# Units of two head pairs over 256 tokens in a delta-rule recurrence, with the triangular inverse's steps on GpSimd

## The chip, the core and the metric

The kernel runs on one core of one Trainium2 chip. The metric is the device time of one execution in microseconds (us). TensorE (PE) multiplies matrices, VectorE (DVE) and ScalarE (ACT) work element by element and evacuate PSUM, GpSimd (POOL) works on SBUF alone here, and SyncE (SP) issues nearly all DMAs, in the order of its queue.

## The reference, cut to what matters

One transformer block over 1024 tokens of width 1024: a modulated norm, one wide projection `u @ w_in`, two mixers (softmax attention with forget gates, 8 heads of 64; and a delta-rule recurrence, "RWKV-7", 8 heads of 64), gates, an output projection and a convolutional FFN. The change touches the recurrence alone:

```python
def step(state, inp):                      # per head: state is 64 x 64
    r_t, w_t, k_t, v_t, a_t, b_t = inp     # a = -kk, b = kk * a_h, kk normalised per head
    sa = jnp.einsum('bhvk,bhk->bhv', state, a_t)
    state = state * w_t[:, :, None, :] + sa[..., None] * b_t[:, :, None, :] + v_t[..., None] * k_t[:, :, None, :]
    y_t = jnp.einsum('bhvk,bhk->bhv', state, r_t)
    return state, y_t
...
_, y = lax.scan(step, state0, ...)         # over 1024 tokens
y = groupnorm(y) * ln_w + ln_b
return (y + sum(r * k * r_k) * v) * g
```

## The kernel before

Everything is held as (channel, token): 128 partitions are two heads (a pair p, p = 0 to 3), and a tile is 128 x 512 (512 tokens, half hf = 0 or 1). The recurrence is cut into chunks of 64 tokens (CH). Inside a chunk it becomes a few small products and the inverse of a unit triangular 64 x 64 matrix; between chunks only the 64 x 64 state is carried on. Eight chunks of one pair (512 tokens, NCU = 8) make a unit, and there are 8 units, (p, hf) with hf inner.

`pre` (L814) readies a unit. It loads the decays (`cum`) and rates (`al`), takes the key norm by a product with a block matrix (`head_sums`, L779: the upper part `hi` is rounded on ACT, the lower part `lo` subtracted on POOL at L782, then two 512 wide matmuls), scans and exponentiates the decays (`el`, `en`), forms the operands `ar` and `bk`, multiplies them into the chunk matrices (`p`, masked into `E` at L878), and sends the 32 x 32 diagonal blocks through DRAM (`sm`) into `M32`, with 128 blocks on 128 partitions. `inverse` (L787) then solves all of them at once: 31 steps of two element-wise VectorE instructions each, a product (L795) and a sum (L799), every one needing the one before. Two DMA legs (`se`, `TT`) bring the result back.

`main` (L924) waits for that (L936 transposes `TT` on VectorE; the products `xi` and `zi` need it first on TensorE), builds `Wt`, `Zt` and `Mt`, and runs the state chain (L989 to L1002): for each of 8 chunks two matmuls of the old state into `sp`, one VectorE instruction (L996) that makes the new state S, two matmuls of the old state into `yp`. A group norm over the heads and the output follow.

The order on TensorE is written by the program itself, through a small planner (`Weave`, L48). A chain yields the time that it must wait, and the planner fills that time with plain 128 x 128 x 512 matmuls from a queue of independent work: the projections of the r, k, v of the pairs to come (`ps_rkv`), queries and keys (`qk`), values (`v`), and 16 gate tiles (`gt`, each two halves of 24 matmuls). Such an item loads its weights on SP (L258), splits them into two parts (L266 on ACT, L270 on VectorE), and its result is evacuated by ACT and VectorE (L383 for r, k and v). In the recurrence the order of the other engines is set by the scheduler. The gate tiles that the recurrence has not used go into the attention that follows (`rk_ps`), and what is left after it is run before the branch products (`br`, L1352).

The numbers that a chain yields are the planner's own: `ready` (L891) is how long after its M32 loads a unit's inverse is taken to be there, 1150 the distance of two state steps, 3400 that from `hi` and `lo` to their matmuls.

Of the kernel before, what the change touches and what calls it, by code (L numbers as in the profile page):

```python
# [9 lines left out]
F32 = mybir.dt.float32  # L10
# [125 lines left out]
def hybrid_block(ctx: ExitStack, tc: tile.TileContext, a, out):  # L136
# [223 lines left out]
    with ExitStack() as es:  # L360
# [26 lines left out]
        def rkv_items(p, hf):  # L387
            ts_ = {x: rkp.tile([128, NH], F32, tag=f"{x}{hf}", name=f"{x}{p}{hf}") for x in "rkv"}
            rkv[p, hf], got[p, hf] = [ts_[x] for x in "rkv"], 0

            def steps(w, x, t):
                if hf == 0:
                    last_col[p, x] = shp.tile([128, 1], F32, tag=f"pv{x}", name=f"pv{p}{x}")
                yield from shifted(w, t, hf, ts_[x], last_col[p, x], f"rkv{t}")
                got[p, hf] += 1

            for x, t in (("k", 4 + p), ("r", p), ("v", 8 + p)):
                yield (lambda t=t: w_in(12 + t)), (lambda w, x=x, t=t: steps(w, x, t))
# [253 lines left out]
        with tc.tile_pool(name="lg", bufs=1, reuse_waits="tile") as lg, \  # L652
# [47 lines left out]
            def lora_chain():  # L700
                yield 13000
                for p in range(4):
                    yield from lora(p, [(j, [(w2h[:, j * 512 : j * 512 + 512], xs2[j]), (w2l[:, j * 512 : j * 512 + 512], xs2[j])], None, b) for j, b in enumerate(("w0", "a0"))])
                use_ln_exp(last[0])
                prods = split_g()
                yield from forget()
                mod_out(2)
                next(mods, None), next(mods, None)
                for p in range(4):
                    yield from lora(p, [(2, prods, None, None)])  # L710
                mod_out(5)
                while got[0, 0] < 3:
                    weave.step()
                yield 0
# [47 lines left out]
            weave.first.extend([*rkv_items(0, 0), *rkv_items(0, 1)])  # L762
# [9 lines left out]

        BKS = (slice(0, 2), slice(1, 3))
# [5 lines left out]
        def head_sums(ps, x, hi, lo):  # L779

            nc.scalar.copy(hi, x)
            nc.gpsimd.tensor_tensor(lo, x, f32(hi), op=ALU.subtract)  # L782
            yield 3400
            mm(ps, blk_r, hi, start=True, stop=False)
            mm(ps, blk_r, lo, start=False, stop=True)

        def inverse(n, M32, TT, chunk_tile, tmp):  # L787
# [3 lines left out]
            t32 = tmp("t32", 256)  # L791
            for s in range(31):
                J, W = s // 4 + 1, 31 - s
                tv = t32[:, 0 : J * W].rearrange("p (j w) -> p j w", w=W)
                i = tt(tv, E32[:, 0:J, s : s + 1].to_broadcast([128, J, W]),  # L795
                   M32[:, s : s + 1, s + 1 : 32].to_broadcast([128, J, W]), op=ALU.mult)
                if s == 0:
                    behind(i)
                tt(E32[:, 0:J, s + 1 : 32], E32[:, 0:J, s + 1 : 32], tv, op=ALU.add)  # L799
# [14 lines left out]
        def pre(k, p, hf):  # L814

            n = f"{p}_{hf}"
            cs = slice(hf * NH, hf * NH + NH)
            rr, kk, vv = rkv[p, hf]
# [8 lines left out]
            nc.sync.dma_start(cum, d_lora[0, p, :, cs])  # L827
            al = tmp("al")
            nc.sync.dma_start(al, d_lora[1, p, :, cs])
            ksq = tmp("ksq")  # L830
            nc.scalar.activation(ksq, kk, AF.Square, scale=V("k_k", p))
            parts = rw.tile([128, 3, NH], F32R, tag="bk", name=f"kp{n}")
            yield 1275 if p + hf else 6000
# [12 lines left out]
            stt(kr, rn, 1e12, kk, op0=ALU.min, op1=ALU.mult)  # L846
# [8 lines left out]
            tt(ar[:, 1], c3(rr), el[:, :, 1:], op=ALU.mult)  # L855
            ts(al, al, V("k_a", p), oka[:, p : p + 1], op0=ALU.mult, op1=ALU.add)
            tt(al, al, kk, op=ALU.mult)
            tt(bk[:, :, 1, :], c3(al), c3(en), op=ALU.mult)
            pcd = chunk_tile("pcd", 3, NCU)
            nc.gpsimd.tensor_copy(pcd, el[:, :, CH])  # L860
            rkb = tmp("ksq")
            stt(rkb, rr, V("r_k", p), al, op0=ALU.mult, op1=ALU.mult)
# [26 lines left out]
            for g in range(4):  # L889
                nc.sync.dma_start(M32[g * 32 : g * 32 + 32, :, :], sm.rearrange("h c b s t -> (h c b) s t"))  # L890
            ready = weave.now + (47500 if k == 0 else 38500)  # L891
            TT = chunk_tile("TT", 2, NCU, CH)
            weave.spawn(inverse(n, M32, TT, chunk_tile, tmp), 8500)

            vt, at = gen(f"vt{n}"), gen(f"at{n}")
            for b in range(4):
                bs = slice(b * 128, b * 128 + 128)
                transpose(vt[:, bs], vv[:, bs], ident)
                transpose(at[:, bs], ar[:, 0, 2 * b : 2 * b + 2, :], ident)
# [21 lines left out]
            tt(bon, bp, vv, op=ALU.mult)  # L921
            units[p, hf] = dict(ready=ready, pcd=pcd, ar=ar, E=E, QA=QA, TT=TT, bon=bon, UV=UV)

        def main(k, p, hf):  # L924
            o = units.pop((p, hf))
            n = f"{p}_{hf}"
            cs = slice(hf * NH, hf * NH + NH)
# [52 lines left out]
            S0 = state.get(p)  # L980

            for c in range(NCU):
                alone = hf == 0 and c == 0
# [5 lines left out]
            for c in range(NCU):  # L989
                if S0 is not None:  # L990
                    for h in range(2):
                        mm(sp[HS[h], c, :], Mt[HS[h], c, :], S0[HS[h], :], start=False, stop=True, more=True)
                S1 = None
                if not (hf == 1 and c == NCU - 1):
                    S1 = rw.tile([128, CH], F32, tag="state", name=f"S{n}{c}", bufs=3)
                    ts(S1, sp[:, c, :], pcd[:, c : c + 1], None, op0=ALU.mult)  # L996
                if S0 is not None:
                    for h in range(2):
                        mm(yp[HS[h], c, :], S0[HS[h], :], Zt[HS[h], c, :], start=False, stop=True, more=True)
                if c + 1 < NCU:  # L1000
                    yield 1150
                S0 = state[p] = S1  # L1002
# [20 lines left out]
            stt(y, y, V("ln_w", p), rs, op0=ALU.mult, op1=ALU.mult)  # L1023
            stt(y, y, V("ln_b", p), bon, op0=ALU.add, op1=ALU.add)
            gg = rw.tile([128, NH], F32, tag="Wt", name=f"gg{n}", bufs=1)
            nc.sync.dma_start(gg, d_lora[2, p, :, cs])
            ov = rw.tile([128, NH], F32, tag="ysq", name=f"o{n}", bufs=1)
            tt(ov, y, gg, op=ALU.mult)
            nc.sync.dma_start(d_orw[p, :, cs], ov)
# [25 lines left out]
        order = [(p, hf) for p in range(4) for hf in range(2)]  # L1055
        passed.update((k, x) for k in (-1, -2) for x in range(2))

        def pre_chain():
            for k, (p, hf) in enumerate(order):
                while got[p, hf] < 3:  # L1060
                    weave.step()
                yield from pre(k, p, hf)
                if p < 3:
                    weave.first.extend(rkv_items(p + 1, hf))
                yield 0

        def main_chain():
            for k, (p, hf) in enumerate(order):
                while (p, hf) not in units:
                    yield 200  # L1070
                yield from main(k, p, hf)
                yield 0
# [1036 lines left out]
```

## Time and profile before

| | before |
|---|---|
| median of 3 runs (lowest to highest) | 1659.14 us (1657.43 to 1660.03) |
| the profiled execution | 1663.44 us, span 1661.7 us |
| VectorE busy | 1202.9 us, 72% |
| ScalarE busy | 809.2 us, 49% |
| GpSimd busy | 136.6 us, 8% |

The recurrence runs from about 165 us to 612 us of the span, attention from there to about 812 us, then the gates that are left, the branches and the FFN. A timeline row has the start and the length in us, the engine, the line, the operation, and what was written from what; matmuls of fp32 operands are two passes and count twice in the profile. A bracket at its end gives idle time of that engine just before, and what ended it. The end of a matmul is modelled, so rates are read from start to start.

### The profile page before, as it was taken

The numbers are of one execution on the slowest core, as the hardware profiler recorded it, in microseconds if no ns is written. First come the engines' busy times: TensorE is split into PE (matmuls) and PEld (weight loads), VectorE is DVE, ScalarE is ACT, GpSimd is POOL, SyncE is SP. The second block draws the span as 40 slices with busy tenths as digits, with TensorE's granted clock in tenths as the row PEclk, the third lists the DMA queues.
The fourth block names the chain that finished last, engine by engine and source line by source line (L and its number), as shares of the span: only waits on it lengthen the run. The fifth ranks groups of instructions, "written<-read, shape, count | busy, mean of one in ns | idle before, by whom it ended". The sixth has DMA issues, their size and how long they took to land.

```text
span 1661.7 us, 25960 instructions
## 1 busy us (share of the span) xinstructions
PE 1621.0 (98%) x9756; PEld 1329.5 (80%) x9756; DVE 1202.9 (72%) x2350; ACT 809.2 (49%) x1473; POOL 136.6 (8%) x169
## 2 busy tenths in 40 slices
PE   7999999999999998999999999999999999999998
PEld 5777877887877777887788888888888888888886
DVE  6875877887886536866579445897777777786677
ACT  7663434443446556665513144654444444555455
POOL 0010101211101020222022000000000000000000
PEclk8999999999999999999999999999999999999999
DMA  9587644443433246542487310243223223574463
GB/s 347 191 308 221 159 131 127 131 125 91 116 101 87 92 156 136 152 119 84 143 284 270 146 73 36 70 138 104 95 96 120 96 95 108 202 272 153 127 209 108
DMA packets 123902, 241.72 MB, mean 145 GB/s; under 512 B 39816, under 2 KB 48320, under 8 KB 123776
## 3 DMA queue, kind: packets, MB, share of 16 engines
q1 hardware_dynamic: 114944, 220.94, 41.1%
q0 software_dynamic: 7600, 17.25, 3.8%
q10 hardware_dynamic: 1232, 1.86, 0.4%
q8 instruction: 77, 1.26, 0.3%
q14 instruction: 49, 0.40, 0.1%
HBM read 174.43 MB, written 65.56 MB: 144 GB/s over the span
## 4 chain that ended last, share of the span: by engine, by line
PE 82%; DVE 8%; ACT 4%; DMA 3%; issue 2%; SPq 0%; POOL 0%; ACTq 0%; DVEq 0%; POOLq 0%
PE X L144 13%; PE D L144 13%; PE Y L144 6%; PE gt L144 6%; PE ps_rkv L144 5%; PE wo L144 5%; PE br L144 5%; PE W L144 3%; PE rk_ps L144 3%; PE qk L144 3%; PE v L144 3%; PE low L144 1%; PE lg L144 1%; PE ov L144 1%; PE sp L144 1%
## 5 line engine op out<-in xcount | busy, mean ns | idle before, releaser
L144 PE MATMUL D<-op,op 128*128 128x512 f32 x924 | 209.8, 390 | 0.0
L144 PEld LDWEIGHTS D<-op,op 128*128 128x128 f32 x924 | 173.4, 188 | 36.2 <-DVE op L1372 0.3
L144 PE MATMUL X<-T_m,S 128*128 128x512 f32 x440 | 107.3, 390 | 0.1
L144 PEld LDWEIGHTS X<-T_m,S 128*128 128x128 f32 x440 | 82.5, 188 | 18.2 <-ACT T_m L1797 0.6
L1371 ACT CAST op<-g 128x512 fp32r<-128x512 f32 x77 | 47.8, 621 | 72.1 <-PE D L144 48.2
L1372 DVE TENSOR_TENSOR op<-g,op 128x512 fp32r<-128x512 f32 x77 | 53.0, 689 | 40.9 <-ACT op L1371 40.8
L1608 DVE SCALAR_TENSOR_TENSOR c<-ab,vec,c 128x512 f32<-128x512 f32 x88 | 65.9, 750 | 19.5 <-ACT c L1611 17.9
L1220 DVE TENSOR_TENSOR tl<-tp,th 128x512 fp32r<-128x512 f32 (+1 forms) x80 | 50.3, 633 | 29.0 <-ACT th L1215 28.4
L1572 DVE TENSOR_TENSOR S<-ur,S 128x512 fp32r<-128x512 f32 x66 | 45.5, 691 | 35.6 <-ACT S L1568 35.4
L270 DVE TENSOR_TENSOR lo_in<-raw_in,hi_in 128x512 fp32r<-128x512 f32 x84 | 58.0, 729 | 16.4 <-PE gt L144 7.5
L1568 ACT CAST S<-ur 128x512 fp32r<-128x512 f32 x66 | 41.0, 622 | 55.6 <-DVE ur L1561 30.6
L1572 DVE TENSOR_TENSOR A<-ur,A 128x512 fp32r<-128x512 f32 x64 | 44.1, 689 | 30.9 <-ACT A L1568 30.7
L266 ACT CAST hi_in<-raw_in 128x1024 fp32r<-128x1024 f32 x42 | 43.9, 1048 | 46.1 <-PE ps_rkv L144 26.2
L795 DVE TENSOR_TENSOR t<-E,M 128x60 f32<-128x60 f32 (+24 forms) x248 | 55.0, 222 | 11.9 <-DMA M<-sm 5.9
L144 PE MATMUL Y<-T_h,A 128*128 128x512 f32 x264 | 63.5, 390 | 0.0
L144 PE MATMUL Y<-T_h,S 128*128 128x512 f32 x264 | 63.3, 390 | 0.0
L799 DVE TENSOR_TENSOR E<-E,t 128x60 f32<-128x60 f32 (+24 forms) x248 | 56.9, 230 | 5.8
L144 PE MATMUL X<-B_b,A 128*128 128x512 f32 x252 | 60.8, 390 | 0.0
L144 PE MATMUL W<-B_f,A 128*128 128x512 f32 x252 | 60.6, 390 | 0.0
L1156 ACT ACTIVATE P<-lg,nm 128x896 f32<-128x896 f32 (+3 forms) x64 | 47.4, 743 | 24.4 <-DVE nm L1147 21.2
L144 PEld LDWEIGHTS Y<-T_h,A 128*128 128x128 f32 x264 | 49.6, 188 | 10.3
L144 PEld LDWEIGHTS Y<-T_h,S 128*128 128x128 f32 x264 | 49.6, 188 | 10.3
(493 smaller groups left out, 4076.9 us busy)
## 6 DMA issues: line engine op xcount, KB each, us to landing
raw_in<-in_w_in SPq DMA_DIRECT2D x50, 512.0 KB
wm<-in_w_mod SPq DMA_DIRECT2D x48, 512.0 KB
ur<-in_w_up SPq DMA_DIRECT2D x44, 512.0 KB
g<-d_g SPq DMA_DIRECT2D x35, 512.0 KB
d_g<-gs SPq DMA_DIRECT2D x44, 256.0 KB
d_g<-c SPq DMA_DIRECT2D x33, 256.0 KB
d_st<-qh SPq DMA_DIRECT2D x64, 128.0 KB
d_gate<-gs SPq DMA_DIRECT2D x32, 256.0 KB
```

The lines of the kernel that those rows point to most:

```text
L144: weave.last = nc.tensor.matmul(o, lhsT, rhs, start=start, stop=stop, skip_group_check=more)
L266: i = nc.scalar.copy(hi, raw)
L270: nc.vector.tensor_tensor(lo[:, c : c + NH], raw[:, c : c + NH], f32(hi[:, c : c + NH]), op=ALU.subtract)
L795: i = tt(tv, E32[:, 0:J, s : s + 1].to_broadcast([128, J, W]), M32[:, s : s + 1, s + 1 : 32].to_broadcast([128, J, W]), op=ALU.mult)
L799: tt(E32[:, 0:J, s + 1 : 32], E32[:, 0:J, s + 1 : 32], tv, op=ALU.add)
L1156: nc.scalar.activation(e[:, 0:n], lg[:, 0:n], AF.Exp, bias=nm[:, 0:1], accum_out=total)
L1220: tt(tl[:, 0:w], tp[:, 0:w], f32(th[:, 0:w]), op=ALU.subtract)
L1371: nc.scalar.copy(hi, src)
L1372: tt(lo, src, f32(hi), op=ALU.subtract)
L1568: nc.scalar.copy(hi, src)
L1572: tt(lo, src, f32(hi), op=ALU.subtract)
L1608: stt(c, ab[:, x + hf * NH : x + hf * NH + NH], V("conv_w", 22 * x + i), c, op0=ALU.mult, op1=ALU.add)
```

## The change

A unit becomes two pairs (2g and 2g + 1) over 256 tokens, so that it still has 8 chunks of 64: chunks 0 to 3 of the first pair, 4 to 7 of the second. There are again 8 units, (g, quarter). Loads and stores take both pairs (two pieces of 256 columns), and instructions whose per-channel factor differs by pair are issued twice with half the width. The state chain takes both pairs in one step: 4 steps of 8 matmuls and one VectorE instruction on 128 x 128. The 62 steps of an inverse are issued to GpSimd; the lower parts in `head_sums` go to VectorE. `ready` is 50000 instead of 38500 (47500 for the first unit stays). The r, k and v tiles hold two pairs by 512 tokens, one buffer each: an item that would overwrite one holds the planner's filler back until the tile was given free.

```diff
+        free = set("krv")
+        def rkv_items(g, hf, x):
             def steps(w, p, t):
+                if p % 2 == 0:
+                    while x not in free:
+                        weave.hold = weave.now + 200
+                        yield
+                    free.remove(x)
+                    rkv[g, hf, x] = rkp.tile([128, 2, NH], F32, tag=x, name=f"{x}{g}{hf}")
...
         def head_sums(ps, x, hi, lo):
             nc.scalar.copy(hi, x)
-            nc.gpsimd.tensor_tensor(lo, x, f32(hi), op=ALU.subtract)
+            tt(lo, x, f32(hi), op=ALU.subtract)
...
             for s in range(31):
                 J, W = s // 4 + 1, 31 - s
-                i = tt(tv, E32[:, 0:J, s : s + 1].to_broadcast([128, J, W]),
+                i = nc.gpsimd.tensor_tensor(tv, E32[:, 0:J, s : s + 1].to_broadcast([128, J, W]),
                    M32[:, s : s + 1, s + 1 : 32].to_broadcast([128, J, W]), op=ALU.mult)
-                tt(E32[:, 0:J, s + 1 : 32], E32[:, 0:J, s + 1 : 32], tv, op=ALU.add)
+                nc.gpsimd.tensor_tensor(E32[:, 0:J, s + 1 : 32], E32[:, 0:J, s + 1 : 32], tv, op=ALU.add)
...
-            stt(ar[:, 0], c3(kr), nkk[:, p : p + 1], el[:, :, 0:CH], op0=ALU.mult, op1=ALU.mult)
-            stt(kr, kr, V("k_k", p), al, op0=ALU.mult, op1=ALU.mult)
+            for j, p in pairs:
+                stt(ar[:, 0, four(j)], c3(kr)[:, four(j)], nkk[:, p : p + 1], el[:, four(j), 0:CH], op0=ALU.mult, op1=ALU.mult)
+            for j, p in pairs:
+                stt(j2(kr)[:, j], j2(kr)[:, j], V("k_k", p), j2(al)[:, j], op0=ALU.mult, op1=ALU.mult)
...
-            ready = weave.now + (47500 if k == 0 else 38500)
+            ready = weave.now + (47500 if k == 0 else 50000)
...
-            for c in range(NCU):
+            for i in range(4):
                 if S0 is not None:
-                    for h in range(2):
-                        mm(sp[HS[h], c, :], Mt[HS[h], c, :], S0[HS[h], :], start=False, stop=True, more=True)
+                    for j in range(2):
+                        for h in range(2):
+                            mm(sp[HS[h], 4 * j + i, :], Mt[HS[h], 4 * j + i, :], S0[HS[h], j, :], start=False, stop=True, more=True)
...
-                    ts(S1, sp[:, c, :], pcd[:, c : c + 1], None, op0=ALU.mult)
+                    tt(S1, sp[:, i::4, :], pcd[:, i::4].unsqueeze(2).to_broadcast([128, 2, CH]), op=ALU.mult)
...
-                if c + 1 < NCU:
-                    yield 1150
+                if i < 3:
+                    yield 1300
...
-        order = [(p, hf) for p in range(4) for hf in range(2)]
+        order = [(g, quarter) for g in range(2) for quarter in range(4)]
```

The order on TensorE in the first unit's state chain, before: each `sp` and `yp` row of one pair, with plain matmuls between.

```order
453 L144 MATMUL sp_0_2294<-S_00_2364,Mt_0_2270 64x64 x2
454 L144 MATMUL yp_0_2293<-Zt_0_2269,S_00_2364 64x64 x2
455 L144 MATMUL ps_rkv_2361<-u_lo,hi_in_2249 128x512 x6
456 L144 MATMUL sp_0_2294<-S_01_2374,Mt_0_2270 64x64 x2
457 L144 MATMUL yp_0_2293<-Zt_0_2269,S_01_2374 64x64 x2
```

The same place of the change:

```order
455 L144 MATMUL sp_0_2294<-S_00_2368,Mt_0_2270 64x64 x4
456 L144 MATMUL yp_0_2293<-Zt_0_2269,S_00_2368 64x64 x4
457 L144 MATMUL qk_0_2365<-u_lo,hi_in_2249 128x512 x7
458 L144 MATMUL sp_0_2294<-S_01_2381,Mt_0_2270 64x64 x4
459 L144 MATMUL yp_0_2293<-Zt_0_2269,S_01_2381 64x64 x4
```

A step has twice the small matmuls and 7 plain ones behind it instead of 6; a unit has 4 steps instead of 8.

The queue of SP in the third unit, before: the stores of query and key tiles (`d_st`) and weight loads (`raw_in`, `raw_v`) that stand between that unit's M32 loads (row 140) and the first leg `se` behind its inverse.

```order
148 L413 DMA d_st<-qh_1_2796 64x512
149 L258 DMA raw_in_3102<-in_w_in 128x1024
150 L1026 DMA gg_1_3226<-d_lora 128x512
151 L413 DMA d_st<-qh_0_2951 64x512 x4
152 L413 DMA d_st<-ql_0_2953 64x512 x2
153 L413 DMA d_st<-qh_1_3010 64x512 x4
154 L413 DMA d_st<-ql_1_3012 64x512 x2
155 L258 DMA raw_v_3162<-in_w_v 128x1024
156 L829 DMA al_0_3426<-d_lora 128x512
157 L802 DMA se_0_2747<-E_0_2682 256x1x32 x4
```

The same unit's leg in the change, whose M32 loads are row 137:

```order
145 L420 DMA d_st<-qh_1_2876 64x512 x3
146 L420 DMA d_st<-ql_1_2878 64x512 x2
147 L420 DMA d_st<-qh_1_2876 64x512
148 L258 DMA raw_in_3093<-in_w_in 128x1024
149 L420 DMA d_st<-qh_0_2982 64x512 x4
150 L822 DMA se_2_2778<-E_2_2713 256x1x32 x4
151 L420 DMA d_st<-ql_0_2984 64x512 x2
152 L829 DMA TT_2_2562<-se_2_2778 32x8x32 x4
153 L420 DMA d_st<-qh_1_3039 64x512 x4
154 L420 DMA d_st<-ql_1_3041 64x512 x2
```

The leg stands one half item of `qk` and a weight load earlier in the queue, ahead of two rows of stores that it came after before.

The end of attention on TensorE, before: the last attention product (`ov`), the gates that are left, the first branch product.

```order
2194 L144 MATMUL ov<-tl_22_9126,vh_8515 128x256
2195 L144 MATMUL rk_ps<-u_hi,lo_in_8583 128x512 x5
2196 L144 MATMUL rk_ps<-u_hi,hi_in_8921 128x512 x8
2197 L144 MATMUL rk_ps<-u_lo,hi_in_8921 128x512 x8
2198 L144 MATMUL rk_ps<-u_hi,lo_in_8922 128x512 x8
2199 L144 MATMUL rk_ps<-u_hi,hi_in_8921 128x512 x8
2200 L144 MATMUL rk_ps<-u_lo,hi_in_8921 128x512 x8
2201 L144 MATMUL rk_ps<-u_hi,lo_in_8922 128x512 x8
2202 L144 MATMUL br_00_9270<-fx_6889,hi_br_9223 128x512
```

The same place of the change:

```order
2108 L144 MATMUL ov<-th_22_9172,vh_8570 128x256
2109 L144 MATMUL ov<-th_22_9172,vh_8570 128x128
2110 L144 MATMUL ov<-tl_22_9177,vh_8570 128x128
2111 L144 MATMUL ov<-tl_22_9177,vh_8570 128x256
2112 L144 MATMUL rk_ps<-u_hi,lo_in_8638 128x512 x2
2113 L144 MATMUL br_00_9262<-fx_6914,hi_br_9215 128x512
```

One gate tile (48 plain matmuls) that stood behind attention stands in the recurrence now: of the items' plain matmuls 1824 lie ahead of attention instead of 1776.

More of the change, by code (lines that the diff above doesn't have):

```diff
@@ L711, in lora_chain @@
                 mod_out(5)
-                while got[0, 0] < 3:
+                while min(got.get((0, 0, x), 0) for x in "krv") < 2:
                     weave.step()
@@ L979, in main @@
             sp = py.tile([128, NCU, CH], F32, tag="sp", name=f"sp{n}")
-            S0 = state.get(p)
+            S0 = state.get(g)
             for c in range(NCU):
-                alone = hf == 0 and c == 0
+                alone = quarter == 0 and c % 4 == 0
                 for h in range(2):
```

130 lines of the change are left out of this document (80 added, 50 removed).

## Prediction, on record before the run

> **What bounds the kernel now.** I read the page first: busy shares and the chain that ended last.
>
> ```profile
> span 1661.7 us, 25960 instructions
> PE 1621.0 (98%) x9756; PEld 1329.5 (80%) x9756; DVE 1202.9 (72%) x2350; ACT 809.2 (49%) x1473; POOL 136.6 (8%) x169
> PE 82%; DVE 8%; ACT 4%; DMA 3%; issue 2%; SPq 0%; POOL 0%; ACTq 0%; DVEq 0%; POOLq 0%
> ```
>
> TensorE carries the end almost alone. Next the table by stage, of which the recurrence is one row (the stretch in us, its length, then the busy time of each engine).
>
> ```profile
> core 0: us, PE busy (x) PEld busy (x) DVE busy (x) ACT busy (x) POOL busy (x), PEclk, DMA share, GB/s
> 165.00:612.00 447.00, 442.65 (x4198) 356.73 (x4198) 330.26 (x942) 205.15 (x360) 58.23 (x74) 1.00 0.41 115
> ```
>
> In the recurrence TensorE is idle 447.00 - 442.65 = 4.4 us, VectorE 117 us. So relieving VectorE is worth at most a few us there, unless TensorE's own work gets cheaper. Two waits of TensorE in this stage (us in total, times, longest):
>
> ```profile
> PE qk L144 <- DVE v L383: 2.4, 1, 2.4
> PE q L144 <- DVE QA L905: 0.4, 1, 0.4
> ```
>
> A busy TensorE can still be a slow one, so I read the timeline of a state step from start to start, the group of the stage that it belongs to (with 1.0 us of waits for the new state S), and a plain run:
>
> ```profile
> 247.52 0.33 PE L144 MATMUL sp<-S,Mt 64*64 64x64 f32 x4
> 247.68 0.28 PE L144 MATMUL yp<-Zt,S 64*64 64x64 f32 x4
> 247.90 1.67 PE L144 MATMUL ps_rkv<-u_lo,hi_in 128*128 128x512 f32 x6
> 249.50 0.33 PE L144 MATMUL sp<-S,Mt 64*64 64x64 f32 x4
> ```
>
> ```profile
> L144 PE MATMUL sp<-S,Mt 64*64 64x64 f32 x240 | 19.9, 243 | 1.3 <-DVE S L996 1.0
> ```
>
> ```profile
> 306.77 2.00 PE L144 MATMUL ps_rkv<-u_hi,lo_in 128*128 128x512 f32 x8
> 308.60 0.62 PE L144 MATMUL ps_rkv<-u_hi,hi_in 128*128 128x512 f32 x2
> ```
>
> A plain matmul costs (308.60 - 306.77) / 8 = 0.229 us. A step lasts 249.50 - 247.52 = 1.98 us: six plain ones are 1.37, the eight small passes 0.32 (0.16 a group, by the first two rows). That leaves **0.29 us a step**, in which TensorE counts as busy and nothing waits: the price of going from 128-row to 64-row matmuls and back.
>
> **The change, part by part.**
>
> *State chain.* The planner's steps with an old state are 60 now (the x240 passes of `sp<-S` are four a step) and 30 then (3 + 4 + 4 + 4 for each of two groups), each with twice the small passes. The small work stays; 30 changes of shape go: 30 x 0.29 = **-8.7 us**. Were the price one of each pair's matmuls rather than of the change of shape, it would be 0; those are the bounds. I take the whole, since the small passes themselves run at 0.04 us each, one behind the other.
>
> *Waits on VectorE.* The steps L795 and L799 leave it:
>
> ```profile
> L795 DVE TENSOR_TENSOR t<-E,M 128x60 f32<-128x60 f32 (+24 forms) x248 | 55.0, 222 | 11.9 <-DMA M<-sm 5.9
> L799 DVE TENSOR_TENSOR E<-E,t 128x60 f32<-128x60 f32 (+24 forms) x248 | 56.9, 230 | 5.8
> L270 DVE TENSOR_TENSOR lo_in<-raw_in,hi_in 128x512 fp32r<-128x512 f32 x62 | 43.7, 743 | 12.7 <-PE gt L144 7.5 <-ACT hi_in L266 3.5 <-PE ps_rkv L144 0.9
> L974 DVE TENSOR_TENSOR Zt<-mz,ar 128x256 f32<-128x256 f32 x16 | 6.7, 422 | 6.1 <-PE mz L144 5.8
> L855 DVE TENSOR_TENSOR ar<-r,el 128x512 f32<-128x512 f32 x7 | 4.8, 691 | 0.1
> L996 DVE TENSOR_SCALAR S<-sp,pcd 128x64 f32<-128x64 f32 x60 | 16.9, 281 | 19.9 <-PE sp L144 19.6
> ```
>
> That takes off 111.9 us. The 32 lower parts add 32 x 0.691 = 22 us, and the six instructions a unit that are split by pair 48 x (2 x 0.422 - 0.691) = 7 us. VectorE then has some 247 us of work in 447, so it binds less. Of the 3.8 us of waits I take **-2.5 us**: the 2.4 us came in the first unit, where VectorE stood behind the inverse's last transfer:
>
> ```profile
> 173.65 0.19 DVE L795 TENSOR_TENSOR t<-E,M 128x31 f32<-128x31 f32 x1 [5.88 <-DMA M<-sm]
> 207.78 0.17 DVE L799 TENSOR_TENSOR E<-E,t 128x8 f32<-128x8 f32 x1
> 214.16 0.43 DVE L936 STREAM_TRANSPOSE X<-TT 32x256 f32<-32x256 f32 x1 [3.81 <-DMA TT<-se]
> 216.31 1.49 PE L144 MATMUL qk<-u_hi,hi_in 128*128 128x512 f32 x4 [2.43 <-DVE v L383]
> ```
>
> Bounds: -3.8 (all go), and +1 (the lower parts, now queued on VectorE behind loads' splits, come late for `mu` or `ssq` as often as S did). The distance from `sp` to the next `sp` grows to 7 x 0.229 + 0.64 + 0.29 = 2.5 us, while S takes some 0.3, so S should not be late again. The splits, the half-size DMAs and ScalarE's second square lie on engines with idle time; were that cover gone, the splits' 7 us are the most they cost.
>
> *The inverse on GpSimd.* No 128x60 instruction of its kind is in the trace; the nearest rows are
>
> ```profile
> L782 POOL TENSOR_TENSOR Mts<-ysq,Zts 128x512 fp32r<-128x512 f32 x8 | 10.4, 1300 | 28.4 <-ACT Zts L781 28.4
> L1264 POOL TENSOR_TENSOR o<-o,R 128x256 f32<-128x256 f32 x12 | 8.5, 726 | 28.5 <-DVE lg L1146 12.4 <-DVE nm L1147 11.7 <-DMA R<-d_rs 4.4
> ...
> 763.47 0.61 POOL L1267 CAST fx<-o 128x512 fp32r<-128x512 f32 x1
> 764.16 1.42 POOL L1270 TENSOR_TENSOR fx<-o,fx 128x256 fp32r<-128x256 f32 x2
> ```
>
> A straight line through 1300 ns at 512 and 726 ns at 256 columns has 2.24 ns a column and 152 ns at none; a dependent pair has 0.08 us between. The loop's sizes sum to 2 x 1560 columns, so a chain is 3120 x 2.24 ns + 62 x (152 + 80) ns = 7.0 + 14.4 = **21.4 us**, from below. Against it stands that the two engines shut each other out:
>
> ```profile
> 283.92 0.69 DVE L855 TENSOR_TENSOR ar<-r,el 128x512 f32<-128x512 f32 x1
> 284.02 0.65 POOL L860 COPY pcd<-el 128x8 f32<-128x8 f32 x1 [8.08 <-ACT el L839]
> ...
> 221.12 0.19 POOL L860 COPY pcd<-el 128x8 f32<-128x8 f32 x1 [8.25 <-ACT el L839]
> L799 DVE TENSOR_TENSOR E<-E,t x248: 149/214/1312, 173.9 to 556.7; 128x60 f32<-128x60 f32 x12, 128x54 f32<-128x54 f32 x8, 128x66 f32<-128x66 f32 x8, 128x28 f32<-128x28 f32 x8
> ```
>
> The same copy took 0.19 us alone and 0.65 beside an instruction that reads two SBUF tensors, and a 0.2 us step of the inverse once took 1.31, as long as a GpSimd subtraction. If every step waited out such an instruction, a chain would last 21.4 + 62 x 0.69 = 64 us, from above. A dozen such instructions a unit (8 x 12 x 0.69 = 66 us), the lower parts (22) and the splits of loads (44) keep VectorE 132 of 447 us, or 30%; a step that falls into one waits half of it, 0.35 us: 62 x 0.30 x 0.35 = 6.5. I take **28 us**, near the lower end, because most steps meet VectorE in other work.
>
> (The Trainium skill, SBUF — State Buffer, section "SBUF: two separate sides", calls the pair of ports that VectorE and GpSimd share an exclusive lock, held for a whole instruction. By that rule the collisions are worth the same 6.5 us, and the rows agree. The Trainium skill's GPSIMD Engine Reference, section "Engine selection", advises against GpSimd for element-wise work as about twice slower with two inputs, which speaks against this change: an estimate from it, twice VectorE's 62 x 0.226 us, is again 28 us.)
>
> What is that allowed? In the first unit the chain began at 173.65 and ended at 207.95, its transfers took 6.2 us, and L936 had no time to spare: 34.3 us. In the third unit:
>
> ```profile
> 267.46 0.18 DVE L795 TENSOR_TENSOR t<-E,M 128x31 f32<-128x31 f32 x1
> 299.24 2.56 SPq L802 DMA_DIRECT2D se<-E  x4
> 310.07 0.89 DVE L936 STREAM_TRANSPOSE X<-TT 32x256 f32<-32x256 f32 x2
> ...
> SPq L802 <- DVE E L799: 20.0, 6, 6.6
> ```
>
> From 267.46 to 310.07 are 42.6 us, less 6.2: 36.4; the change puts 162 plain matmuls instead of 144 between that unit's `p` and `xi`, +4 us, so 40. The tighter place is SP's queue. Stores and weight loads stand behind `se`, and it stands about 7 us of TensorE's work earlier than before (the half item of 24 plain ones is 5.5): 31.8 - 7 = 25 us behind the start. SP has waited up to 6.6 us at `se` without a wait on TensorE that I can put to it. So up to about 25 + 6.6 = 32 us cost nothing, and 28 do: **0**.
>
> *The gate tile that moves.* 48 plain matmuls leave this place:
>
> ```profile
> 812.37 1.32 PE L144 MATMUL rk_ps<-u_hi,lo_in 128*128 128x512 f32 x5
> 814.38 2.14 PE L144 MATMUL rk_ps<-u_hi,hi_in 128*128 128x512 f32 x8 [0.69 <-ACT gs L1295]
> 826.41 1.98 PE L144 MATMUL br<-fx,hi_br 128*128 128x512 f32 x8
> 815.50 1.14 ACT L1344 CAST hi_br<-raw_br 128x512 fp32r<-128x512 f32 x2
> ```
>
> From 814.38 to 826.41 are 12.0 us, and they cost 48 x 0.229 = 11.0 in the recurrence. But they covered ScalarE's cast of the branch weights, done at about 816.1, so the first `br` comes 1.7 us after 814.38 instead of at once: -12.0 + 11.0 + 1.7 = **+0.7 us** (from -1, cast early, to +3, GpSimd's lower part late too).
>
> *Sum.* -8.7 - 2.5 + 0 + 0.7 = -10.5: span 1661.7 - 10.5 = 1651.2. The profiled execution took 1663.44 with its ends, 4.3 above the median of the runs; off the median, 1659.1 - 10.5 = **1648.6, say 1649 us**.
>
> **The rivals.**
>
> 1. *GpSimd's chain is too slow* (slower). From 32 us on, SP holds the loads and stores at `se`, and each us is paid in each of 8 units; at 33.3 us the gain is gone. A step of 0.56 us, between 0.345 alone and 1.03 always shut out, makes 34.7 us: 8 x 2.7 = 21.6, so 1649 + 22 = 1671. For it: the collisions above, and the self-wait between steps. Against it: most rows of GpSimd that ran alone.
> 2. *The change of shape is paid per pair*, so that doubling the step saves nothing: -2.5 + 0.7, so 1657, within the bound. A chain of 33 us ends there as well. For it: no row shows a step of 16 small passes.
> 3. *Shape price saved, but the lower parts and S come late on VectorE*: -8.7 + 1 + 0.7, so 1652; still faster.
>
> **How the numbers follow.** Forecast 0.55; rival 3 0.13; rival 2 0.12; rival 1 0.20. A measurement tells about 0.2%, 3.3 us, from no change: faster is the forecast and rival 3, less a little for chains near 33 us, 0.67; same 0.13; slower 0.20. The low end has all 3.8 us of waits gone and the cast early, less the 1.3 us by which single runs lie around their median: 1659.1 - 8.7 - 3.8 - 1 - 1.3 = 1644; the high end goes a little past rival 1's price, 1673, since a chain can be longer still.
>
> **What would show it.** In the changed profile: the time from `sp` to the next `sp` should be 2.5 us with 7 plain matmuls; 30 such steps; GpSimd's chain 25 to 32 us from first to last step; no wait on TensorE for `xi`, `zi` or a weight split; `br` idle 1 to 3 us at its start. Wrong would be: chains of over 33 us, SP waiting at `se` over 7 us, steps of over 2.6 us.

## The result: slower, and the profile after

The changed kernel takes 1676.84 us (median of 4 runs, 1673.46 to 1677.94) against 1659.59 before; the ratio on record is **1.0084, 95% interval 1.0067 to 1.0101**. (The two medians alone give 1.0104; the record does not show how its ratio weighs the runs, and either way the change is slower.) The prediction said 1649 us, and at most 1673. Forecast faster, it came out slower.

The page's first part, the changed kernel (busy time, share of the span, instructions):

```profile
span 1675.2 us, 25974 instructions
PE 1615.9 (96%) x9756; PEld 1330.6 (79%) x9756; DVE 1126.0 (67%) x1906; ACT 811.7 (48%) x1485; POOL 263.7 (16%) x633
```

TensorE is busy 5.1 us *less* than before and the span is 13.5 us longer, so TensorE's idle time has grown by 18.6 us. Work was saved, and more than that was lost in waiting. What TensorE waited for, from 165 to 660 us (total, times, longest):

```profile
PE ps_rkv L144 <- DVE ql L416: 7.0, 1, 7.0
PE rk_ps L144 <- ACT gs L1345: 4.7, 1, 4.7
PE zi L144 <- ACT X L993: 3.7, 1, 3.7
PE ps_rkv L144 <- DVE r L383: 3.3, 1, 3.3
PE sp L144 <- DVE S L1047: 2.1, 3, 1.0
```

Three long stalls are new, and the one at `rk_ps` was 1.2 us before. For their places, cut the span at three instructions that every kernel has: the first step of the inverse, the first `rk_ps` matmul (the attention begins) and the first `br` matmul (the branches begin). The tenth gate tile, 48 matmuls or 11.0 us, lies in the recurrence after the change and in the attention before; I count it to the attention in both. All numbers are us, worked out from the timelines:

```
                          before   changed   difference
to the inverse's start    173.65    171.63     -2.0
recurrence, tile out       441.7     449.8     +8.1
attention, tile in         211.1     218.5     +7.4
branches to the end        835.3     835.4      0
```

The first row varies by over 3 us between kernels that do the same there, and the last by over 5; the two in the middle are the change. The prediction's terms for them were -8.7 - 2.5 = -11.2 and +0.7.

**The recurrence.** The table by stretches (length, busy time of PE, PEld, DVE, ACT and POOL, granted clock, DMA share, GB/s) for the whole of it, before and after:

```profile
173.65:615.34 441.69, 437.34 (x4135) 352.51 (x4134) 330.37 (x940) 202.87 (x354) 60.29 (x78) 1.00 0.40 114
171.63:632.39 460.76, 442.57 (x4185) 363.39 (x4184) 254.04 (x490) 208.34 (x369) 193.72 (x545) 0.99 0.40 114
```

Less the 11.0 us of the moved tile TensorE is busy 431.6 us instead of 437.3, and idle 18.2 instead of 4.4. SyncE's waits at the stores of the inverse's result (`se`, now L822):

```profile
SPq L822 <- POOL E L819: 60.7, 7, 13.7
SPq L822 <- POOL el L874: 9.7, 1, 9.7
```

70.4 us in eight units, 20.0 before. The third unit shows what hangs on it. From the timelines of GpSimd, SyncE, VectorE and TensorE (start, duration; in brackets the idle time before it and what ended it):

```profile
273.50 0.24 POOL L815 TENSOR_TENSOR t<-E,M 128x31 f32<-128x31 f32 x1 [23.22 <-DMA M<-sm]
301.51 0.21 POOL L819 TENSOR_TENSOR E<-E,t 128x8 f32<-128x8 f32 x1
289.68 2.37 SPq L420 DMA_DIRECT2D d_st<-qh  x4
301.75 2.56 SPq L822 DMA_DIRECT2D se<-E  x4
304.41 1.20 SPq L420 DMA_DIRECT2D d_st<-ql  x2
307.50 0.69 DVE L416 SCALAR_TENSOR_TENSOR ql<-qk,qh 128x512 fp32r<-128x512 f32 x1 [8.30 <-DMA d_st<-ql]
308.25 1.65 PE L144 MATMUL ps_rkv<-u_hi,hi_in 128*128 128x512 f32 x3 [7.01 <-DVE ql L416]
```

GpSimd's chain runs from 273.50 to 301.72, 28.2 us; the page's groups give its two operations (busy us, mean ns):

```profile
L815 POOL TENSOR_TENSOR t<-E,M 128x60 f32<-128x60 f32 (+24 forms) x248 | 85.8, 346 | 124.2 <-DMA M<-sm 105.8
L819 POOL TENSOR_TENSOR E<-E,t 128x60 f32<-128x60 f32 (+24 forms) x248 | 89.2, 360 | 19.0
```

SyncE has nothing left ahead of `se` at 292.05, 18.6 us behind the chain's start, and stands there for 9.7 us. The store of an unrelated `ql` is behind `se`; until it lands the next `ql` has no buffer, VectorE waits 8.3 us for it, TensorE 7.0 us for the PSUM tile. The first unit's two stalls are of the same make: a weight load (`raw_in`) and the decays (`cum`) stood behind `se` until 207.66 and 214.86.

After a long stall TensorE is also slower for a while. From the same table by stretches:

```profile
300.00:308.00 8.00, 1.23 (x6) 0.69 (x4) 0.50 (x1) 1.72 (x3) 1.88 (x9) 0.80 0.29 58
308.00:311.00 3.00, 2.75 (x7) 1.81 (x9) 3.00 (x6) 0.21 (x1) 0.00 (x0) 0.50 0.74 166
311.00:314.00 3.00, 3.00 (x24) 2.57 (x23) 2.09 (x6) 1.50 (x3) 0.00 (x0) 0.89 0.93 203
314.00:318.00 4.00, 4.00 (x30) 3.11 (x29) 3.03 (x6) 1.05 (x1) 0.00 (x0) 1.00 0.92 335
```

The granted clock is 0.50 for 3 us behind the stall and 0.89 for 3 more, which costs 3 x 0.50 + 3 x 0.11 = 1.8 us beyond the stall itself.

**The attention.** Its first late gate (a gate tile left over for the attention, `rk_ps`) waits for a buffer, that is for an old gate's store to land (ScalarE's timeline, first row), and at its end `br` waits for ScalarE's cast (TensorE's, second row; ScalarE's, last two):

```profile
643.39 1.28 ACT L1345 ACT_TABLE_LOAD   x1 [3.49 <-DMA d_gate<-gs]
839.85 3.01 PE L144 MATMUL br<-fx,hi_br 128*128 128x512 f32 x8 [3.92 <-issue]
837.84 1.28 ACT L205 ACT_TABLE_LOAD   x1
839.13 1.14 ACT L1394 CAST hi_br<-raw_br 128x512 fp32r<-128x512 f32 x2
```

The table load of 1.28 us, which in the kernel before comes behind this cast (at 827.98 us), stands ahead of it now.

### The profile page after: what moved, and what is told of

It is laid out like the page before. It is cut to its first block, busy times and chain, and to the rows that moved or that the text cites. A ratio compares the mean times of both kernels' runs of the same rounds, so it can differ in the third digit from the quotient of the medians.

```text
span 1675.2 us, 25974 instructions
## 1 busy us (share of the span) xinstructions
PE 1615.9 (96%) x9756; PEld 1330.6 (79%) x9756; DVE 1126.0 (67%) x1906; ACT 811.7 (48%) x1485; POOL 263.7 (16%) x633
## 4 chain that ended last, share of the span: by engine, by line
PE 78%; POOL 6%; DVE 4%; DMA 4%; ACT 3%; issue 2%; SPq 1%; ACTq 0%; POOLq 0%; DVEq 0%
PE X L144 13%; PE D L144 13%; PE gt L144 7%; PE Y L144 6%; PE wo L144 5%; PE br L144 5%; PE ps_rkv L144 5%; PE W L144 3%; POOL E L819 3%; POOL t L815 3%; PE rk_ps L144 3%; PE qk L144 2%; PE v L144 2%; PE low L144 1%; PE ov L144 1%
## 5 line engine op out<-in xcount | busy, mean ns | idle before, releaser
L815 POOL TENSOR_TENSOR t<-E,M 128x60 f32<-128x60 f32 (+24 forms) x248 | 85.8, 346 | 124.2 <-DMA M<-sm 105.8
L144 PEld LDWEIGHTS X<-T_m,S 128*128 128x128 f32 x440 | 82.4, 188 | 18.2 <-ACT x L1698 0.6
L819 POOL TENSOR_TENSOR E<-E,t 128x60 f32<-128x60 f32 (+24 forms) x248 | 89.2, 360 | 19.0
L144 PE MATMUL ps_rkv<-u_hi,hi_in 128*128 128x512 f32 x192 | 53.1, 409 | 11.4 <-DVE ql L416 7.0
L1206 ACT ACTIVATE P<-lg,nm 128x896 f32<-128x896 f32 (+3 forms) x64 | 47.5, 742 | 24.0 <-DVE nm L1197 21.2
```

Source lines behind the costliest of these rows:

```text
L144: weave.last = nc.tensor.matmul(o, lhsT, rhs, start=start, stop=stop, skip_group_check=more)
L815: i = nc.gpsimd.tensor_tensor(tv, E32[:, 0:J, s : s + 1].to_broadcast([128, J, W]), M32[:, s : s + 1, s + 1 : 32].to_broadcast([128, J, W] ...
L819: nc.gpsimd.tensor_tensor(E32[:, 0:J, s + 1 : 32], E32[:, 0:J, s + 1 : 32], tv, op=ALU.add)
L1206: nc.scalar.activation(e[:, 0:n], lg[:, 0:n], AF.Exp, bias=nm[:, 0:1], accum_out=total)
```

## The experiments

The ratios are to the kernel before on the same chip. `rec` and `att` are the two middle rows of the table above, from one profiled execution each. `rec` repeats to 0.4 us where two kernels do the same there (before and e12, e4 and e9, e5 and e10). A dip of the clock, which follows some short stalls and not others, moves either column by about 1.7 us (see the last section):

```
                                        us     ratio and interval         rec     att
before                                                                  441.7   211.1
changed                            1676.84  1.0084 (1.0067-1.0101)      449.8   218.5
e1  inverse on VectorE             1668.89  1.0037 (1.0021-1.0053)      441.2   219.8
e2  se later in SP's queue         1670.14  1.0053 (1.0039-1.0066)      442.2   217.7
e3  before + inverse on GpSimd     1679.45  1.0110 (1.0096-1.0124)      458.7   210.8
e4  se and TT on GpSimd's queue    1658.86  0.9983 (0.9974-0.9993)      432.8   215.1
e5  e4 + gate tile held            1659.44  0.9991 (0.9978-1.0005)      433.1   217.3
e6  units of two pairs alone       1665.90  1.0036 (1.0023-1.0048)      437.7   216.5
e7  e3 + se, TT on GpSimd's queue  1680.13  1.0121 (1.0107-1.0134)      461.0   211.3
e8  e4 + lower parts on GpSimd     1689.13  1.0174 (1.0161-1.0187)      462.9   216.6
e9  e4 + third head's loads later  1655.12  0.9959 (0.9945-0.9974)      432.4   212.3
e10 e5 + third head's loads later  1655.23  0.9961 (0.9948-0.9975)      433.3   214.6
e11 e4 with units of one pair      1666.56  1.0021 (1.0009-1.0034)      446.5   213.8
e12 before + third head's later    1663.51  1.0014 (1.0003-1.0024)      441.6   212.1
```

### e1: the inverse back on VectorE

```diff
-                i = nc.gpsimd.tensor_tensor(tv, E32[:, 0:J, s : s + 1]...
+                i = tt(tv, E32[:, 0:J, s : s + 1]...
...
-                nc.gpsimd.tensor_tensor(E32[:, 0:J, s + 1 : 32], ...
+                tt(E32[:, 0:J, s + 1 : 32], ...
```

> The changed kernel with the 62 steps of the inverse back on VectorE; units of two pairs and the head sums' lower parts on VectorE stay. Theory 1 (SyncE's queue stands at `se` while GpSimd's chain runs, and loads and stores behind it come late): the three stalls of TensorE in the recurrence (3.3, 3.7 and 7.0 us) and the slow TensorE clock after them (about 1.7 us each) go, SP waits under 25 us in all at `se`; 14.0 + 5 us less than the changed kernel, some 1658 us. Rival 2 (the units of two pairs themselves make loads and buffers late): the stalls stay, 1672 us or more. Rival 3 (VectorE with the 62 steps and the lower parts is late with S and the weight splits): the long stalls go but waits on VectorE of 5 us or more come, 1662 to 1668 us.

1668.89 us. The stalls of 7.0 and 3.3 us are gone, that at `zi` is 1.8, and SyncE's wait at `se` is 7.8 us in all, as theory 1 has it; but TensorE's waits in this run come close to the sign of rival 3 (5 us on VectorE):

```profile
PE sp L144 <- DVE S L1047: 4.9, 4, 1.6
PE zi L144 <- ACT X L993: 1.8, 1, 1.8
```

VectorE is late with `S`, for 4.9 us in all. The recurrence is 8.6 us shorter than in the changed kernel, where theory 1 alone had 19: TensorE's idle time falls from 18.2 to 8.9 us, but the slow clock stays. It loses 6.0 us of the recurrence here and 5.1 in the changed kernel (busy time times one less the granted clock, summed over stretches of 2 us), although no wait in this recurrence is longer than 1.8 us.

### e2: the stores of `se` later in SyncE's queue

```diff
+            yield 25000
             se = scr.tile([2, NCU, 2, 32, 32], F32, tag="se", name=f"se{n}")
             for g in range(4):
-                nc.sync.dma_start(se..., E32...)
+                behind(nc.sync.dma_start(se..., E32...))
```

> The changed kernel, the inverse on GpSimd, but the stores of its result (`se`) are ordered behind the matmul that stands 25 us of the plan after the chain's start, so that loads and stores go ahead of them on SyncE's queue. Theory 1: SP's waits at `se` fall from 70 us to under 25, the stalls before `ps_rkv` and `zi` go though the chain still takes 28 us: some 1658 us. Rival 2 (the two-pair units): stays at 1672 or more. Rival 4 (the chain itself is too long for `xi`, whatever the queue): new waits of TensorE at `xi` through the transposes of `X`, 1670 us or more.

1670.14 us, a half success: the stalls at 212, 221 and 301 us are gone, but SyncE still waits 31 us at `se`, in one unit longer than ever, and others appear (TensorE's waits in the last two rows, and one of 2.4 us at `S`):

```profile
SPq L825 <- POOL el L874: 17.8, 1, 17.8
SPq L825 <- POOL E L819: 13.3, 5, 7.7
PE at L151 <- DVE E L922: 5.9, 1, 5.9
PE sp L144 <- DVE Mt L1025: 2.8, 1, 2.8
```

No new wait at `xi`: rival 4 falls. A place in an in-order queue that suits one unit does not suit the next.

### e4: the inverse's transfers on GpSimd's own queue

```diff
-                nc.sync.dma_start(
+                nc.gpsimd.dma_start(
                     se.rearrange(...)[:, g, :, :], E32[g * 32 : g * 32 + 32, :, :])
...
-                    nc.sync.dma_start(TT[r0 : r0 + 32, ...
+                    nc.gpsimd.dma_start(TT[r0 : r0 + 32, ...
```

> The changed kernel with the inverse's two transfers (`se` and `TT`) issued by GpSimd behind its own chain instead of by SyncE. Theory 1: SP has no wait at `se` at all and the three stalls go, unless GpSimd, which now issues eight DMAs a unit and waits for the first four to land, is late with the decays `el` and `pcd` of the next unit: 1655 to 1662 us. Rival 2: 1672 us or more. If GpSimd becomes the one that is late: waits of ScalarE at `el`, 1665 to 1680 us.

1658.86 us. This decides it. The chain is as long as ever, 28.8 us in the third unit, yet the recurrence is 432.8 us, **17.0 less than in the changed kernel and 8.9 less than before**. What is left of TensorE's waits in the recurrence:

```profile
PE sp L144 <- DVE S L1047: 3.4, 3, 1.6
PE ps_rkv L144 <- DVE r L383: 1.8, 1, 1.8
PE zi L144 <- ACT X L993: 1.1, 1, 1.1
```

Neither GpSimd's speed nor the units of two pairs made the recurrence slow, but eight DMAs a unit at the wrong queue. No stretch of it has a lowered clock any more. The attention is still 4.0 us longer than before.

### e3 and e7: only the inverse on GpSimd, with units of one pair

In e3 the kernel before has the two `tt` of the inverse on `nc.gpsimd` and nothing else; e7 moves the transfers there too, as e4 does.

> The kernel before, with the inverse's 62 steps on GpSimd and nothing else: units of one pair, head sums' lower parts on GpSimd. Theory 1: SP comes to `se` some 9 us before the chain's end in most units here too, and TensorE stalls for 10 to 20 us in the recurrence: 1670 to 1680 us. Rival 2 (the stalls belong to the two-pair units): within 3 us of before, 1657 to 1663. If VectorE's relief counts and nothing else does: 1655 to 1657.

> As e3_before_inverse_gpsimd (units of one pair), with the inverse's two transfers issued by GpSimd behind its chain. Theory 1: SP does not wait at `se`, and most of the 15 us that e3 lost in the recurrence come back: 1660 to 1666 us. Rival 9 (in e3 it was not SP's queue but GpSimd's own: lower parts, decays and memsets that stand in line behind the chain): stays at 1674 or more.

e3 took 1679.45 us, as theory 1 expected, and SyncE stands 59.0 us at `se` in it. But **the queue is not the whole reason**: e7, where SyncE has no `se` at all, took 1680.13. As rival 9 has it, GpSimd's own line is too long there, since the lower parts of the head sums stand in it. What SyncE's waits alone cost in e3 stays open, since TensorE's waits are not the same ones in the two runs (for the lower parts 0.9 us in e3, 7.1 in e7). e7's longest sum of waits:

```profile
PE mu L144 <- POOL Mtr L782: 7.1, 3, 3.6
```

### e8 and e6: the lower parts back on GpSimd, with and without the inverse there

```diff
-            tt(lo, x, f32(hi), op=ALU.subtract)
+            nc.gpsimd.tensor_tensor(lo, x, f32(hi), op=ALU.subtract)
```

e8 is e4 with this line; e6 is the changed kernel with this line and the inverse on VectorE (e1's edit).

> As e4_se_on_gpsimd_queue, with the head sums' lower parts back on GpSimd: the third part of the change undone. If they queue behind the chain (28 us) and the waits for `se`, TensorE waits at `ssq`, `bs`, `mu` and `va`: 5 us and more in several units, 1670 us or more. If GpSimd has room for them between the steps: within 3 us of e4, 1656 to 1662.

> The changed kernel with the inverse on VectorE and the head sums' lower parts on GpSimd, as before: only the units of two pairs are left of the change. Theory 7 (30 instead of 60 steps of the state chain save 8.7 us of TensorE, and in e1 waits on VectorE, whose load the lower parts raise, took most of that back): the recurrence is 6 to 9 us shorter than before, the attention 4 to 9 us longer by the moved tile: 1655 to 1662 us, under e1's 1669. Rival 8 (units of two pairs need GpSimd's inverse: VectorE's bursts are what makes S late, with or without the lower parts): waits at S of 5 us and more remain, 1665 to 1670.

e8 took 1689.13 us: with the chain on GpSimd, the lower parts there cost 30.1 us of recurrence. TensorE's longest sum of waits in it:

```profile
PE mu L144 <- POOL Mtr L802: 15.3, 5, 6.3
```

So the part of the change that the prediction counted as 22 us of VectorE's time is what makes a chain on GpSimd possible. e6 took 1665.90 us, which is rival 8's time without its sign: TensorE waits 2.6 us for `S`, not 5. The recurrence is 4.0 us shorter than before, where theory 7 had 6 to 9. TensorE's busy time, less the moved tile, is 9.2 us less than before (428.1 against 437.3; 1.6 of this is a dip of the clock that only the kernel before has), so most of theory 7's saving is there; its idle time is 5.2 us more (9.6 against 4.4), in short waits at `S`, `zi`, `at` and others.

e6 against e1 is the test of the lower parts beside an inverse on VectorE, and no difference shows: 1.0036 and 1.0037 of before. That e6's profiled recurrence is 3.5 us shorter than e1's does not count against this, since the slow clock takes 6.0 us of e1's and nothing of e6's.

### e11: units of one pair, all else as in e4

The kernel before with the edits of e3, the transfers on GpSimd's queue and the lower parts on VectorE.

> As e4_se_on_gpsimd_queue (inverse and its transfers on GpSimd, lower parts on VectorE), but with the kernel before's units of one pair: what the units of two pairs are worth when the rest is the same. Theory 7 (0.29 us a step of the state chain, 30 steps fewer: 8.7 us): the recurrence is some 9 us longer than in e4, the attention 4 us shorter: 1662 to 1666 us. Rival 2 of the prediction (the price of a change of shape is paid per pair): the recurrence as in e4, the attention 4 us shorter, 1654 to 1656 us.

1666.56 us; the recurrence is 13.7 us longer than in e4. One stall of 5.5 us at `tb`, in the first unit, is in this. TensorE's idle time is 1.5 us more than in e4 (8.2 against 6.7), and the slow clock behind that stall costs 3.5; the other 8.7 us are the units. The price of a step can be read directly, in the last unit of e11 and of e4 (TensorE's timeline):

```profile
591.00 0.33 PE L144 MATMUL sp<-S,Mt 64*64 64x64 f32 x4
591.16 0.28 PE L144 MATMUL yp<-Zt,S 64*64 64x64 f32 x4
591.37 1.65 PE L144 MATMUL gt<-u_hi,lo_in 128*128 128x512 f32 x6
592.96 0.33 PE L144 MATMUL sp<-S,Mt 64*64 64x64 f32 x4
```

```profile
590.20 0.40 PE L144 MATMUL yp<-Zt,S 64*64 64x64 f32 x8
590.53 1.89 PE L144 MATMUL gt<-u_hi,lo_in 128*128 128x512 f32 x7
592.35 0.45 PE L144 MATMUL sp<-S,Mt 64*64 64x64 f32 x8
592.63 0.40 PE L144 MATMUL yp<-Zt,S 64*64 64x64 f32 x8
592.96 1.89 PE L144 MATMUL gt<-u_hi,hi_in 128*128 128x512 f32 x7
594.78 0.45 PE L144 MATMUL sp<-S,Mt 64*64 64x64 f32 x8
```

One pair: 1.96 us, less 6 plain ones of 0.229, leaves 0.59. Two pairs: 2.43 us, less 7 plain ones, leaves 0.83 and not 1.17. That is 0.34 us saved in each of 30 steps, 10 us; the prediction had 0.29 and 8.7. So the units are worth 9 to 10 us by both ways. Rival 2 of the prediction falls.

### e5: the tenth gate tile held back

```diff
-                if not self.loaded:
+                if not self.loaded or (not self.late and not self.first and len(self.queue) <= 6):
                     return False
```

> As e4_se_on_gpsimd_queue, but the planner starts no gate tile in the recurrence after the one that the kernel before ends with, so the tenth tile (48 matmuls) goes back into the attention; 8 of them stood ahead of the last `va`, 40 behind it. In e4 the way from the first `rk_ps` to the first `br` is 204.1 us for 48 matmuls (11.0 us) less than before, where it takes 211.1: 4.0 us lost. Theory 5 (the moved tile takes cover from the attention's start and end): no idle ahead of `br` (3.9 us in e4), the first wait for a gate's buffer back to 1.2 us from 3.5, at most 1.8 us of new wait at `va`; 2 to 4 us less than e4, so 1655 to 1657 us. Rival 6 (the loss in the attention has another cause): the idle times stay and the time is e4's or up to 2 us more.

1659.44 us, no gain over e4. The idle time ahead of `br` is gone and the first late gate waits 1.2 us, as theory 5 says, but the attention starts with other waits (TensorE's and VectorE's timelines; `lg` are the attention's logits, `th` and `tl` the upper and lower part of its weights, `ov` their product with the values):

```profile
609.36 1.76 PE L144 MATMUL lg<-first,first 68*128 68x512 f32 x7 [1.36 <-DMA first<-d_st]
623.29 0.38 PE L144 MATMUL ov<-tl,first 128*128 128x256 f32 x1 [3.02 <-DVE tl L1270]
622.54 0.69 DVE L1270 TENSOR_TENSOR tl<-tp,th 128x512 fp32r<-128x512 f32 x1 [6.90 <-DMA d_orw<-o]
```

VectorE waits for a buffer whose 256 KB store has not landed. In e4 it is a gate's store instead (SyncE's and ScalarE's timelines): two are issued between 614.78 and 620.54, and the buffer comes free at 626.5.

```profile
614.78 5.76 SPq L356 DMA_DIRECT2D d_gate<-gs  x2
626.54 1.28 ACT L1345 ACT_TABLE_LOAD   x1 [2.35 <-DMA d_gate<-gs]
```

Both kernels load three heads of 2.1 MB each at that place (by the page of DMAs 1024 + 544 + 512 KB, so not the 1.5 MB of e9's expectation). That gave the next theory.

### e9, e10 and e12: the third head's loads later

```diff
-                if k % 4 == 1 and h < 7:
-                    load_head(h + 1)
+                if (k == 3 or k % 4 == 1 and k != 5) and h < 7:
+                    load_head(2 if k == 3 else h + 1)
...
+    late = lambda h, x: h == 2 and nc.gpsimd.tensor_copy(x, marks["nm"][:, 0:1])
```

`late` writes one column of each of the third head's three tiles from a row maximum of the first head, so that the loads behind it wait for that maximum. e9 is e4 with this, e10 is e5, e12 the kernel before.

> As e4_se_on_gpsimd_queue, but the loads of the attention's third head (1.5 MB) wait for a row maximum of the first head, some 14 us after the first `rk_ps` instead of 3 us ahead of it. Theory 10 (the attention starts late because these loads hold back the small stores that free a buffer: in e4 a gate's 256 KB store took some 11 us to land and the first late gate waited for it): the wait of 3.5 us and the slow clock behind it go, 2 to 5 us less than e4, 1654 to 1657 us. Rival 11 (the first two heads' loads alone fill the DMA engines, or the stall has another source): within 1.5 us of e4, 1657 to 1661.

> As e5_gate_tile_held (tenth gate tile back in the attention), with the third head's loads delayed as in e9. Theory 10: the waits of e5 at the attention's start (1.4 us for the first head's load, 3.0 us behind a store of `o` that took some 13 us to land) go, at most 1.5 us of them stays; 3 to 6 us less than e5, 1653 to 1656 us. Rival 11: within 1.5 us of e5, 1658 to 1661.

> The kernel before with nothing changed but the third head's loads, delayed as in e9: a control. If the delay helps only where the moved gate tile's store meets these loads: its waits at the attention's start (1.2 us for the first late gate, 2.0 us for a softmax) stay and the time is within 2 us of before. If it helps any version of the kernel: 3 us or more less than before, and then e9's lead over e4 says nothing about the change.

e9 took 1655.12 us: the first late gate waits 1.2 us instead of 3.5, and the attention is 2.8 us shorter than in e4. e10 took 1655.23; its wait of 3.0 us at `ov` is 0.7, while the 1.4 us for the first head's load stays at 1.5. Theory 10 holds in e9. In e10 the time is as it says, but 2.2 us of those waits stay, where it allowed 1.5. The control e12 gained nothing (1663.51, ratio 1.0014), and its two waits stay at 1.2 and 2.0 us, so e9's lead over e4 belongs to the place at which the changed recurrence meets these loads. e9 and e10 are **faster than both kernels**, by 0.4% against the one before.

## Why the prediction was wrong

- **The state chain (-8.7)** was right in its mechanism and a little small: a step saves 0.34 us, not 0.29, or 10 us in 30 steps.
- **VectorE's waits (-2.5)** had the wrong sign. VectorE's load fell as forecast (254 us in the changed recurrence, 247 said), but with the queue cleared (e4) TensorE's idle time in the recurrence is 6.7 us, 4.4 before: the waits at `S` went from 1.0 to 3.4 us, and two of 1.8 and 1.1 us stand where one of 2.4 was. Why `S` is late longer beside a less loaded VectorE stays open. That e4's recurrence is 8.9 us shorter than before, not far from the -11.2 of the two terms, is partly luck: TensorE's busy time fell by 11.2 us, of which 1.6 are the dip of the clock that the kernel before has behind its 2.4 us wait, and its idle time rose by 2.4.
- **GpSimd's chain (28 us)** was right: 22.9 to 33.0 us in the eight units, 28.0 on average. One of its 62 operations took 0.353 us on average, against 0.265 worked out for it alone (7.0 us for the columns and 62 x 0.152), and 28.0 / 62 = 0.45 with the gap, against 0.345 alone and 0.45 with the collisions that the prediction put at 6.5 us.
- **"So up to about 25 + 6.6 = 32 us cost nothing" is the step that failed.** Both numbers were wrong. SyncE came to `se` 19.3, 14.7 and 18.6 us behind the chain's start in the first three units (at 190.91, 232.11 and 292.05), not 25: I had moved its old place by 7 us of TensorE's work, where the rows of the new queue ahead of `se` should have been followed in time (below). And 6.6 us was the longest wait that had cost nothing *before*, with other things behind it in the queue. Waits of 9.9 and 9.7 us in the first and third unit cost 3.3 + 3.7 + 7.0 = 14.0 us of stalls; one of 13.7 us in the second cost none. What a held queue cost here was decided by what stood behind the holder, not by the length of the hold. Rival 1 named this mechanism, but set its threshold at a chain of 32 us and its price at 1 us for each in every unit; neither is so.
- **The clock behind a stall** was no term at all. In the recurrence the three dips cost about 1.7 us each, 5 us: 14.0 and 5 less the 2.9 us of the same waits that e4 keeps are 16, of the 17.0 that e4 gets back.
- **The gate tile (+0.7)** was mis-sized: +7.4 in the changed kernel, +4.0 in e4, +1.2 in e9. It counted 1.7 us of idle time at `br` (3.9 measured, 1.3 of it the table load, and a dip of the clock behind it). It did not see the attention's start, where a store waits beside the heads' loads; e9 shows that for 2.8 us of e4's 4.0. The place of the tile alone is not the cause: with the tile put back (e5) the attention is still 6.2 us longer than before. Some of these differences are the clock's, which lost 3.3 us of the attention before, 5.4 in the changed kernel, 2.6 in e4 and 1.7 in e9.
- **The signs named in advance:** steps of 2.5 us (2.43) and chains of 25 to 32 us held on average; no wait for `zi` and weight splits (3.7 and 3.3 us), `br` idle 1 to 3 us (3.9) and SyncE waiting under 7 us at `se` (up to 13.7) did not. The last was the one to look at first.

The kernel before shows both errors in the 25 (SyncE's timeline in the third unit, whose chain began at 267.46):

```profile
286.29 2.39 SPq L413 DMA_DIRECT2D d_st<-qh  x4
297.35 0.44 SPq L829 DMA_DIRECT2D al<-d_lora  x1
```

The 31.8 us that the prediction started from is the issue of `se` at 299.24. SyncE had nothing left ahead of it at 297.79, 30.3 us behind the start, and stood there for 1.4 us. And the row that stands last ahead of `se` in the new queue, four stores of `qh`, was done at 288.68, 21.2 us behind the start; the 18.6 measured is nearer to that than to 25.

Open: why `S` is late in the units of two pairs, the wait of 1.4 us for the first head's load in e5 and e10, and the idle time at `br` in e9; none was tried on the chip.

## What to carry to other kernels

When work moves to a slower engine, move the DMAs that wait for it to a queue where nothing that is needed soon stands behind them: here eight DMAs a unit decided between a recurrence 8 us longer and one 9 us shorter. With the lower parts in GpSimd's line the same move won nothing (e7 against e3). A wait in an in-order queue is priced by listing what is behind it and who needs that when, not by the longest wait that was harmless before. And parts of a change are not additive: the lower parts on VectorE are worth 30 us once a chain fills GpSimd (e8 against e4), and nothing that the runs can tell while the inverse is on VectorE (e1 against e6).

## What the runs showed of the hardware

The granted clock of TensorE falls behind stalls much shorter than the 7 us above, and their length alone does not decide it. In the recurrences and attentions of the fourteen traces every stall of 2.2 us or more is followed by time at 0.50, the 2.4 us one of the kernel before too. Of the stalls between 1.5 and 2.0 us some are and some are not. The same wait for a gate had no dip behind it in the kernel before (first two rows, TensorE's timeline and the table by stretches, columns as above) and one in the changed kernel (last two):

```profile
791.15 1.66 PE L144 MATMUL rk_ps<-u_hi,hi_in 128*128 128x512 f32 x6 [2.00 <-ACT gs L1295]
791.00:794.00 3.00, 2.85 (x14) 2.26 (x15) 1.73 (x6) 2.48 (x6) 0.00 (x0) 1.00 0.23 87
812.82 2.47 PE L144 MATMUL rk_ps<-u_hi,hi_in 128*128 128x512 f32 x6 [2.00 <-ACT gs L1345]
813.00:816.00 3.00, 3.00 (x9) 2.35 (x10) 1.76 (x5) 2.18 (x5) 0.00 (x0) 0.57 0.23 87
```

So a difference of one dip, some 1.7 us, between two single profiles says nothing about the change.

The Trainium skill, TensorE: Matmul & The Clock Gate, section "Part 1: The HAM clock gate (the "warmup" mystery)", gives a free-running window of some 3.4 us that has to be idle before the clock is halved, and about as much busy time to get it back. The halving agrees, and so does the length: the 1.7 us that most dips cost are 3.4 us at 0.50. The 2.0 us do not fit a window that must be idle throughout, and here the measurement decides.
